# The opening of a two-layer hybrid trunk: first modulation on TensorE, norms applied tile by tile, convolution shifted later

## The chip, the core and the metric

The kernel runs on one core of one Trainium2 chip. The metric is device microseconds for one execution. Engines are called by their names in the profile: PE is TensorE (matmul), DVE is VectorE, ACT is ScalarE, POOL is GpSimd, SP is SyncE, which here only issues DMAs.

## The reference, cut to what matters

The trunk has two layers over 1024 latent tokens and 256 context tokens of 1024 channels. Layer 0 mixes tokens by a Conformer convolution module, layer 1 by attention; each is followed by a SwiGLU block. The change lies in layer 0, up to its second pointwise product.

```python
mod_x = (silu(c) @ w_mod[0] + b_mod[0]); mod_c = silu(c_ctx) @ w_mod[0] + b_mod[0]     # 6 x 1024 each
sh, sc, g, shf, scf, gf = split(mod, 6)                    # per stream
h  = rmsnorm(x, norm_g[0, 0]) * (1 + sc) + sh              # same for ctx with mod_c
u  = h @ w_pw1 + b_pw1                                     # 1024 -> 2048
a, gt = split(u, 2); u = a * sigmoid(gt)
u  = depthwise_conv(u, width 31) + b_dw                    # along the tokens of each stream
u  = silu(layernorm(u, ln_g, ln_b))
y  = u @ w_pw2 + b_pw2
x  = x + g * rmsnorm(y, norm_g[0, 1])
```

## The kernel before

**Tiling.** Channels lie on the 128 partitions, in KT = 8 tiles; tokens lie along the free axis in three pieces, C (256 context tokens), L and R (512 latent tokens each). Every large product runs in three matmuls on operands split in a high and a low part (wh·xh, wh·xl, wl·xh; L403 to L405 in `pw1`). A weight tile of 128x1024 is loaded by an SP DMA (L132), cast to its high part on ACT (L133), and the low part is a subtraction on DVE (L137) or POOL (L139). `split` does the same for activations: ACT L145, DVE L148.

**Opening.** Modulation chunk f is 128 of the 6144 outputs. On PE (`mod_pe`, L209 to L219) a chunk is eight K steps over a raw 512 KB weight tile, then a copy, a small transpose and a bias on ACT. On DVE (`mod_dve`, L226 to L243) a chunk is a multiply-and-reduce of the transposed raw tile (L241) for each of the two streams. Before the first product the kernel needs the chunks k (shift) and 8+k (scale), k = 0..7. It makes the eight shifts and the scale of k = 0 on PE, and the seven other scales on DVE. The raw tiles for PE lie in six slots of the buffers T4 and T5.

**Norms.** `norm_in` squares a piece (on ACT, L294), sums the squares over channels on PE (L297), takes an inverse root on DVE (L279 to L287, after L316), broadcasts it over the partitions by PE transposes (L323), and applies it: DVE L343 scales a tile, ACT L348 adds the shift and rounds to the high part, DVE L349 makes the low part. The three pieces are done one after the other, in program order.

**Blocks.** The loop over k = 0..7 runs `pw1(k)`: for each piece 48 matmuls, a sigmoid on ACT (L411) and a gate on DVE (L412) into `u`. `pw1` yields four times per piece, twelve times per k. After pieces C and R, eight DMAs on SP's queue (L421) regroup `u` into rows of 16 channels by 8 token phases (`U`, in buffer KB), and `split` makes `uh`, `ulo` (buffer HS) from it. The convolution is a generator, `conv`: group q = 8k+g is 15 matmuls of 162 columns (L464) against a weight map that DVE expands one group ahead (L444); three groups share a PSUM bank and are evicted by ACT (L469); after a block's last group two DMAs on ACT's queue store it to DRAM (L473) and DVE adds it into a running sum (L476, L478). Between the yields of `pw1` the loop calls `next(cg)`, from yield 18 on and at two yields of three. What is left of the 64 groups runs after the loop. Other yields step the second modulation (chunks 16 to 47), on DVE.

**Layer norm and pw2.** `ln` loads a piece of the stored convolution (SP, L499), subtracts the mean (PE L487, DVE L503), sums squares, scales (DVE L511), applies Silu (ACT L513). `pw2` (L517 to L529) is the second product; its matmuls stand at L156 to L158.

**What sets the order.** Each engine runs its own queue in order. A scheduler builds the queues from the program order and priorities; `later(n)` sinks PE instructions by n steps. `set_banks` names the PSUM banks of each kind. SP's queue is strictly in order, and a DMA there waits for its buffer ahead of everything behind it. Stores after the convolution, and nothing else in this part, go through ACT's queue.

Of the kernel before, what the change touches and what calls it, by code (L numbers as in the profile page):

```python
# [15 lines left out]
P = 128  # L16
# [17 lines left out]
PE_SCALE = (0,)  # L34
# [21 lines left out]
class Kern:  # L56
# [164 lines left out]

    def mod_dve(self, l, fs, cr, raws, junk):
# [3 lines left out]
        nc.sync.dma_start(cr.rearrange("p s d -> p (s d)"), self.a["crow"].to_broadcast([P, 2048]))  # L226
        nc.scalar.activation(cr, cr, AF.Silu)
# [62 lines left out]
    def sq_pe(self, ps, src, k, n):  # L290

        nc = self.nc
        sq = self.sb(n)
        nc.scalar.activation(sq, src, AF.Square)  # L294
        J = n // P
        for j in range(J):
            nc.tensor.matmul(ps[:, j:j + 1], lhsT=sq[:, j * P:(j + 1) * P], rhs=self.c["ones"],  # L297
                             start=k == 0 and j == 0, stop=k == KT - 1 and j == J - 1)

    def stat(self, acc, n, rs=True, kind="st", sums=None):  # L300
# [4 lines left out]
        ps = self.bank(kind) if sums is None else sums  # L305
        v = self.tiny([P, 16], "nv")
        parts = [(0, n // P, P)] + ([(n // P, J, rem)] if rem else [])
        for j in range(J if sums is None else 0):
# [50 lines left out]
    def norm_in(self, l, src_dram, tags, c0, c1, box, xt=None, kind="st", pe=False):  # L359
# [9 lines left out]
        if pe:  # L369
            ps = self.bank(kind)  # L370
            for k in range(KT):
                self.sq_pe(ps, xt[:, k, :], k, n)
                yield 0.1
            pb = self.stat(None, n, kind=kind, sums=ps)
        else:
            acc = self.acc(n)
            for k in range(KT):
                self.sq_acc(acc, xt[:, k, :], k)
                yield 0.1
            pb = self.stat(acc, n, kind=kind)  # L380
# [9 lines left out]
    def pw1(self, k, hs):  # L390
# [5 lines left out]
        for b, (c0, c1) in PIECES.items():  # L396
# [21 lines left out]
            if b != "L":  # L418
                u0, u1 = (0, CTX) if b == "C" else (CTX, TOK)
                for g in range(CG):  # L420
                    nc.sync.dma_start(self.U[:, g, o:o + nn], u[16 * g:16 * g + 16, u0:u1])  # L421
# [4 lines left out]
            yield  # L426

# [21 lines left out]
    def conv(self):  # L449

        nc, c = self.nc, self.c
        for q in range(KT * CG):
            k, g = divmod(q, CG)
            uh, ul, v = self.uh[k % 2], self.ulo[k % 2], self.v
            self.conv_maps(q + 1)
            h = g % 3
# [14 lines left out]
            if g == CG - 1:  # L471
                for d, o0, nn in ((self.vc[k], 0, NC_), (self.vl[k], 2 + NC_, NL)):
                    nc.scalar.dma_start(d.rearrange("g q n -> q g n"), v[:, :, o0:o0 + nn])  # L473
# [17 lines left out]
    def ln(self, b, ytag, stags, box):  # L491
# [4 lines left out]
        cv = self.T(ytag, [P, KT, n])  # L496
        for k in range(KT):
            d = (self.vc if b == "C" else self.vl)[k].rearrange("g (c s) n -> (g c) (s n)", s=PH)
            nc.sync.dma_start(cv[:, k, :], d[:, 512:] if b == "R" else d[:, :n])  # L499
# [356 lines left out]
    def build(self):  # L856
# [4 lines left out]

        mg = self.mod_dve(0, [8 + k for k in range(KT) if k not in PE_SCALE], *self.mod_room("HS", "KB"))
        gC = self.norm_in(0, a["xT"], ("HR", "T1", "T1"), *PIECES["C"], hs["C"], pe=True)
        self.set_banks(mm=[0, 1, 2], md=[3, 4, 7], st=[5, 6])
        b1 = self.cp.tile([P, KT], F32, tag="b1", name="b1")
        nc.vector.tensor_scalar(out=b1, in0=c["bmod"][:, 0, 8:16], scalar1=1.0, scalar2=None, op0=ALU.add)
# [5 lines left out]
        for k in range(KT):  # L872
# [9 lines left out]
            for s in range(2):  # L882
                if not onpe:
                    next(mg)
# [316 lines left out]
```

## Time and profile before

| | |
|---|---|
| median of 3 runs | 3191.86 us (3185.87 to 3194.25) |
| the profiled execution | 3192.76 us, span 3191.0 us |
| mean granted PE clock | 0.957 |
| busy: PE, DVE, ACT, POOL | 92%, 60%, 37%, 11% of the span |
| share of the chain that ended last | PE 35%, DVE 5%, DMA 2%, ACT 2% |

Times inside an execution are counted from the span's start, which is shorter than the execution's own time by 1.76 us. The layer's convolution module is over at about 600 us of the span; everything after (the rest of layer 0, and layer 1) is the same code in both kernels. A line of the trace's timeline gives the start, the busy time, the engine, the source line, the operation with its tiles, xN where N of them follow one another, and in brackets the idle time ahead of it with what ended it. "PEclk" is the granted clock as a share of full speed.

### The profile page before, as it was taken

The numbers are of one execution on the slowest core, as the hardware profiler recorded it, in microseconds if no ns is written. First come the engines' busy times: TensorE is split into PE (matmuls) and PEld (weight loads), VectorE is DVE, ScalarE is ACT, GpSimd is POOL, SyncE is SP. The second block draws the span as 40 slices with busy tenths as digits, with TensorE's granted clock in tenths as the row PEclk, the third lists the DMA queues.
The fourth block names the chain that finished last, engine by engine and source line by source line (L and its number), as shares of the span: only waits on it lengthen the run. The fifth ranks groups of instructions, "written<-read, shape, count | busy, mean of one in ns | idle before, by whom it ended". The sixth has DMA issues, their size and how long they took to land. (4 is left out here: it accounts for less than half of the span.)

```text
span 3191.0 us, 39121 instructions
## 1 busy us (share of the span) xinstructions
PE 2949.1 (92%) x15231; PEld 2467.8 (77%) x15231; DVE 1907.5 (60%) x3034; ACT 1193.0 (37%) x1859; POOL 354.1 (11%) x188
## 2 busy tenths in 40 slices
PE   7899978899999999999967799998999999899997
PEld 5789977788888887787856577776777778778886
DVE  5777667762333369855475689856656653663335
ACT  4211226432112232233332478754544543332222
POOL 0000000000000012222221100011111112222222
PEclk8899969999999999999988899998999999999998
DMA  6344333422122147623333411122122233343332
GB/s 231 109 130 117 77 103 113 158 86 66 61 66 66 60 154 242 254 94 107 119 111 127 148 53 60 52 90 88 62 80 78 63 103 108 126 145 99 93 99 73
DMA packets 170794, 340.68 MB, mean 107 GB/s; under 512 B 30448, under 2 KB 83824, under 8 KB 169328
## 3 DMA queue, kind: packets, MB, share of 16 engines
q1 hardware_dynamic: 153824, 332.72, 32.3%
q10 hardware_dynamic: 16784, 5.47, 0.7%
q8 instruction: 119, 1.95, 0.3%
q14 instruction: 67, 0.55, 0.1%
HBM read 290.94 MB, written 41.94 MB: 104 GB/s over the span
## 5 line engine op out<-in xcount | busy, mean ns | idle before, releaser
L158 PE MATMUL ps<-T,wl 128*128 128x512 f32 (+1 forms) x2256 | 847.2, 376 | 36.1 <-DVE wl L137 34.7
L156 PE MATMUL ps<-T,wh 128*128 128x512 f32 (+1 forms) x2256 | 847.7, 376 | 11.1 <-ACT wh L133 5.7
L157 PE MATMUL ps<-T,wh 128*128 128x512 f32 (+1 forms) x2192 | 818.9, 374 | 1.4 <-DVE T L148 1.3
L133 ACT CAST wh<-wr 128x1024 fp32r<-128x1024 f32 x348 | 365.4, 1050 | 1078.8 <-PE ps L157 833.5
L139 POOL TENSOR_TENSOR wl<-wr,wh 128x1024 fp32r<-128x1024 f32 x123 | 302.7, 2461 | 2441.6 <-ACT wh L133 2232.3
L137 DVE TENSOR_TENSOR wl<-wr,wh 128x1024 fp32r<-128x1024 f32 x225 | 282.1, 1254 | 403.2 <-ACT wh L133 396.3
L158 PEld LDWEIGHTS ps<-T,wl 128*128 128x128 f32 x2256 | 431.8, 192 | 111.6 <-DVE wl L137 38.2
L156 PEld LDWEIGHTS ps<-T,wh 128*128 128x128 f32 x2256 | 432.1, 192 | 84.3 <-ACT wh L133 5.9
L157 PEld LDWEIGHTS ps<-T,wh 128*128 128x128 f32 x2192 | 419.0, 191 | 71.1 <-DVE T L148 2.8
L157 PE MATMUL ps<-HS,wh 128*128 128x512 f32 (+1 forms) x784 | 308.2, 393 | 3.0 <-DVE HS L148 3.0
L803 DVE TENSOR_TENSOR T<-ps,T 128x512 fp32r<-128x512 f32 x320 | 216.9, 687 | 126.6 <-ACT T L802 125.9
L156 PE MATMUL ps<-HS,wh 128*128 128x512 f32 (+1 forms) x720 | 282.0, 393 | 3.6 <-DVE sm L612 3.6
L158 PE MATMUL ps<-HS,wl 128*128 128x512 f32 (+1 forms) x720 | 282.3, 393 | 3.0 <-DVE wl L137 3.0
L802 ACT CAST T<-ps 128x512 fp32r<-128x512 f32 x320 | 186.1, 586 | 194.2 <-PE ps L799 170.6
L799 PE MATMUL ps<-cst,T 128*128 128x128 f32 x1100 | 193.8, 277 | 30.1 <-DVE T L803 30.0
L636 DVE TENSOR_TENSOR T<-ps,T 128x512 f32<-128x512 f32 (+1 forms) x168 | 110.3, 663 | 159.7 <-PE ps L158 158.9
L799 PEld LDWEIGHTS ps<-cst,T 128*128 128x128 f32 x1100 | 132.7, 142 | 79.8 <-DVE T L803 61.0
L787 DVE TENSOR_SCALAR_CACHE_REDUCE T<-ps,rq 128x1280 f32<-128x1280 f32 x110 | 170.0, 1545 | 30.3 <-PE ps L781 25.4
L612 DVE TENSOR_TENSOR sm<-sm,ps 128x256 f32<-128x256 f32 (+1 forms) x88 | 54.6, 620 | 203.7 <-PE ps L158 203.7
L157 PEld LDWEIGHTS ps<-HS,wh 128*128 128x128 f32 x784 | 149.4, 191 | 34.2 <-DVE HS L148 4.0
L789 ACT ACTIVATE T<-T,mn 128x1280 f32<-128x1280 f32 x110 | 150.4, 1367 | 63.9 <-DVE T L787 63.6
L781 PE MATMUL ps<-KB,q 128*128 128x512 f32 (+1 forms) x576 | 144.0, 368 | 25.8 <-DMA KB<-ksd 16.5
(189 smaller groups left out, 4222.5 us busy)
## 6 DMA issues: line engine op xcount, KB each, us to landing
wr<-in_w SPq DMA_DIRECT2D x264, 512.0 KB
T<-in_wmodT SPq DMA_DIRECT2D x48, 512.0 KB
wr<-in_pw SPq DMA_DIRECT2D x40, 512.0 KB
KB<-in_wmodT SPq DMA_DIRECT2D x19, 512.0 KB
wr<-in_wmodT SPq DMA_DIRECT2D x16, 512.0 KB
wr<-in_wq SPq DMA_DIRECT2D x16, 512.0 KB
qsd<-sb SPq DMA_DIRECT2D x32, 256.0 KB
q<-qsd SPq DMA_DIRECT2D x32, 256.0 KB
```

The source lines that it names most:

```text
L133: nc.scalar.copy(hi, raw)
L137: nc.vector.tensor_tensor(lo, raw, hi.bitcast(F32), op=ALU.subtract)
L139: nc.gpsimd.tensor_tensor(lo, raw, hi.bitcast(F32), op=ALU.subtract)
L156: nc.tensor.matmul(out[:, :n], lhsT=wh, rhs=xh, start=k == 0, stop=False)
L157: nc.tensor.matmul(out[:, :n], lhsT=wh, rhs=xl, start=False, stop=False)
L158: nc.tensor.matmul(out[:, :n], lhsT=wl, rhs=xh, start=False, stop=k == nk - 1)
L781: nc.tensor.matmul(sc[:, k0:k0 + w], lhsT=q[:, h, :], rhs=kt[:, p * TOK + k0:p * TOK + k0 + w], start=p == 0, stop=p == 1)
L787: nc.vector.tensor_scalar(out=pt, in0=sc, scalar1=rq[:, h:h + 1], scalar2=None, op0=ALU.mult, op1=ALU.min, accum_out=mn)
L789: nc.scalar.activation(pt, pt, AF.Exp, bias=mn, scale=-1.0, accum_out=sums[:, 0, h:h + 1])
L799: nc.tensor.transpose(tp[:, h * P:(h + 1) * P], Ps[h][:, j * P:(j + 1) * P], c["ident"])
L802: nc.scalar.copy(ph, tp)
L803: nc.vector.tensor_tensor(pl, tp, ph.bitcast(F32), op=ALU.subtract)
```

## The change

- All sixteen chunks of shift and scale go to PE; their raw tiles lie in ten slots (T4, T5 and KB). No DVE chunk is left ahead of the first product.
- The pieces are loaded in four DMAs each. C's and L's squares and inverse roots are made first; C and L are applied tile by tile as each k's columns come. R's squares lie in between, from k = 4 on. All pieces now sum squares with `sq_acc` (ACT squares, DVE adds, PE sums at the end).
- Of the eight regrouping DMAs of a piece, the four with even g go through ACT's queue, the others through SP's.
- `split_u(k-1)` is called two yields into `pw1(k)`; the convolution starts at yield 22 instead of 18. After the loop three more groups run ahead of the last block's split.
- The convolved pieces are loaded back block by block from inside `conv` (`load_cv`), C's last block directly from SBUF.
- A Silu of one column on ACT stands after the loop. The PSUM banks of layer norm and `pw2` are four each.

```diff
 norm_in:
-        if pe:
-            ps = self.bank(kind)
-            for k in range(KT):
-                self.sq_pe(ps, xt[:, k, :], k, n)
...
+        acc = self.acc(n)
+        for k in range(KT):
+            self.sq_acc(acc, xt[:, k, :], k)
+            yield 0.1
+        pb = self.stat(acc, n, kind=kind)
 pw1:
-                    nc.sync.dma_start(self.U[:, g, o:o + nn], u[16 * g:16 * g + 16, u0:u1])
-            if b == "R":
-                if k + 1 < KT:
-                    self.pre.append(self.wload(a["pw1"][KT + k + 1]))
-                self.split(self.uh[k % 2], self.ulo[k % 2], self.U)
+                    (nc.sync if g % 2 else nc.scalar).dma_start(self.U[:, g, o:o + nn], u[16 * g:16 * g + 16, u0:u1])
+            if b == "R" and k + 1 < KT:
+                self.pre.append(self.wload(a["pw1"][KT + k + 1]))
 conv:
+            if q == CG * (KT - 1):
+                self.cvs = {}
+                for b, t in (("C", "KB"), ("L", "T4"), ("R", "T5")):
+                    self.cvs[b] = self.T(t, [P, KT, PIECES[b][1] - PIECES[b][0]])
+                    for j in range(KT - 1):
+                        self.load_cv(b, j)
 build:
-        mg = self.mod_dve(0, [8 + k for k in range(KT) if k not in PE_SCALE], *self.mod_room("HS", "KB"))
...
+        raws = [self.T(t, [P, 4, 1024]) for t in ("T4", "T5")] + [self.T("KB", [P, 2, 1024])]
+        raws = [raws[i][:, j] for j in range(4) for i in range(3) if j < raws[i].shape[1]]
         for k in range(KT):
             if k == 5:
                 self.pre += [self.wload(a["pw1"][0]), self.wload(a["pw1"][KT])]
+            self.mod_pe(k, raws[2 * k % len(raws)])
+            self.mod_pe(8 + k, raws[(2 * k + 1) % len(raws)])
...
+            if k == 1:
+                load_x("L")
+                self.cond_row(cr)
+                for _ in range(KT + 1):
+                    next(gL)
+                next(gC)
+            if k:
+                next(gC)
+                next(gL)
+            if k == 3:
+                xs["R"] = self.T("HS", [P, KT, 512])
+                load_x("R")
...
+            if k > 3:
+                for _ in range(2):
+                    next(gR)
...
         for k in range(KT):
             for i, _ in enumerate(self.pw1(k, hs)):
-                if 12 * k + i >= 18 and i % 3 != 1:
+                if k and i == 2:
+                    self.split_u(k - 1)
+                if 12 * k + i >= 22 and i % 3 != 1:
                     next(cg)
                 if i % 3 != 2:
                     next(modg, None)
+        self.set_banks(mm=[0, 1, 2, 3], cv=[4, 7], st=[5, 6])
+        nc.scalar.activation(self.tiny([P, 16], "nv")[:, :1], c["ones"], AF.Silu)
+        for _ in range(3):
+            next(cg)
+        self.split_u(KT - 1)
         for _ in cg:
             pass
```

**Where it moves instructions.** The first place is DVE's queue around piece R's inverse root, ahead of `pw1(1)`. Before, from R's sums to its first scaled tiles (nv, nq, nr, nh are the root's small tiles, HS holds R, sb is the scaled tile, HR the gate's result):

```order
L444 TENSOR_TENSOR T_610<-cwin,cst 128x640 x4
L316 TENSOR_SCALAR nv<-ps 128x4
L279 TENSOR_SCALAR nq<-nv 128x4
L283 TENSOR_SCALAR nh<-nv 128x4
L281 TENSOR_SCALAR nr<-nq 128x4
L412 SCALAR_TENSOR_TENSOR HR<-ps,cst,sm 128x512
L343 SCALAR_TENSOR_TENSOR sb<-HS,col_107,ps 128x512
```

The same place now (cwin is the convolution's window weights, T_622 a weight map, T_104 is piece L and T_282 its low part):

```order
L337 SCALAR_TENSOR_TENSOR sb<-T_104,col_109,ps 128x512
L310 TENSOR_SCALAR nv<-ps 128x4
L147 TENSOR_TENSOR cwin<-KB,cwin 128x320
L283 TENSOR_SCALAR nq<-nv 128x4
L287 TENSOR_SCALAR nh<-nv 128x4
L432 TENSOR_TENSOR T_622<-cwin,cst 128x640
L343 SCALAR_TENSOR_TENSOR T_282<-sb,mod_99,T_281 128x512
L285 TENSOR_SCALAR nr<-nq 128x4
L399 SCALAR_TENSOR_TENSOR HR<-ps,cst,sm 128x256
L337 SCALAR_TENSOR_TENSOR sb<-HS,col_109,ps 128x512
```

R's root now starts while piece L is still being scaled, with the window's split, L's last low part, C's gate and six weight maps (one is shown) among its steps; L's gate, which stood ahead of R's first tile, now stands behind R's last.

The second place is ACT's queue at the end of `pw1(0)`. Before, from the first 512-column sigmoid on (T_571 is R's high part, wh a weight's, HS the convolution's input):

```order
L411 ACT_TABLE_LOAD
L411 ACTIVATE sm<-ps,cst 128x512
L348 ACTIVATE T_571<-sb,mod_99 128x512 x8
L133 CAST wh<-wr 128x1024
L145 CAST HS<-KB 128x1328
```

The same place now, where T_584 is R's high part and KB<-HR the regrouping DMA of `u`:

```order
L398 ACTIVATE sm<-ps,cst 128x256
L342 ACTIVATE T_281<-sb,mod_99 128x512
L943 ACT_TABLE_LOAD
L943 ACTIVATE nv<-cst 128x1
L408 DMA KB<-HR 128x1x32 x4
L342 ACTIVATE T_584<-sb,mod_99 128x512 x2
L398 ACT_TABLE_LOAD
L398 ACTIVATE sm<-ps,cst 128x512
L342 ACTIVATE T_584<-sb,mod_99 128x512 x6
L408 DMA KB<-HR 128x1x128 x4
L132 CAST wh<-wr 128x1024
L144 CAST HS<-KB 128x1328
```

The one-column Silu, which the program has after the loop, stands here between C's and L's sigmoids with a table load of its own, and L's sigmoid has another behind it; four regrouping DMAs stand ahead of R's first tile and four ahead of the next weight's cast.

The third place is DVE's queue around the last block's split (HS<-KB), after the last `pw1` matmul. Before, from the last gate of `pw1(7)` on:

```order
L412 SCALAR_TENSOR_TENSOR HR<-ps,cst,sm 128x512
L444 TENSOR_TENSOR T_610<-cwin,cst 128x640 x4
L148 TENSOR_TENSOR HS<-KB,HS 128x1328
L148 TENSOR_TENSOR cwin<-KB,cwin 128x320
L444 TENSOR_TENSOR T_610<-cwin,cst 128x640 x6
L476 TENSOR_REDUCE sm<-HR 128x162
```

And now, from the same gate on:

```order
L399 SCALAR_TENSOR_TENSOR HR<-ps,cst,sm 128x512
L432 TENSOR_TENSOR T_622<-cwin,cst 128x640 x2
L147 TENSOR_TENSOR HS<-KB,HS 128x1328
L432 TENSOR_TENSOR T_622<-cwin,cst 128x640 x8
L147 TENSOR_TENSOR cwin<-KB,cwin 128x320
L432 TENSOR_TENSOR T_622<-cwin,cst 128x640 x6
L477 TENSOR_REDUCE sm<-HR 128x162
```

Two maps make one group. Behind the split stand now eight maps of groups that don't read it, and the window's split after them; on PE sixteen groups instead of thirteen follow the last `pw1` matmul.

More of the change, by code (lines that the diff above doesn't have):

```diff
@@ L495, in ln @@
         n = c1 - c0
[L496 to L499, printed above, removed]
+        cv = self.cvs[b]
         mean = self.mean(b)[:, :n]
@@ L944, in build @@
             pass
-        for _ in self.ln("R", tags["R"][0], tags["R"][1], sv["R"]):
+        for _ in self.ln("R", tags["R"][1], sv["R"]):
             pass
```

99 lines of the change are left out of this document (46 added, 53 removed).

## Prediction

> **What bounds the kernel now.** I read the page first, for what carries the whole.
>
> ```profile
> PE 2949.1 (92%) x15231; PEld 2467.8 (77%) x15231; DVE 1907.5 (60%) x3034; ACT 1193.0 (37%) x1859; POOL 354.1 (11%) x188
> ```
>
> PE is busy 92% of the span, so time can come only from stretches where PE waits or runs at a low clock. The change touches the first 600 us, so next I cut these with the windows view at the marks of the program: start of `pw1(0)`, start of `pw1(1)`, end of the last `pw1` matmul, end of the convolution, start of `pw2`. Columns: stretch, length, busy time of PE, PEld, DVE, ACT, POOL, granted PE clock, DMA share, GB/s.
>
> ```profile
> 0.00:36.29 36.29, 22.23 (x137) 16.36 (x137) 17.54 (x52) 13.95 (x36) 0.20 (x4) 1.00 0.76 282
> 36.29:123.89 87.60, 67.61 (x332) 56.02 (x332) 55.47 (x108) 33.40 (x55) 5.76 (x5) 0.72 0.37 120
> 123.89:409.66 285.77, 284.03 (x1775) 255.61 (x1776) 205.86 (x282) 54.84 (x100) 0.00 (x0) 0.98 0.43 115
> 409.66:449.80 40.14, 34.44 (x195) 33.93 (x194) 21.57 (x26) 6.48 (x15) 0.00 (x0) 0.63 0.55 158
> 449.80:469.90 20.10, 7.39 (x30) 6.48 (x30) 13.87 (x39) 6.90 (x16) 0.00 (x0) 0.50 0.23 66
> 469.90:600.00 130.10, 113.68 (x590) 96.70 (x591) 108.86 (x231) 83.25 (x144) 0.00 (x0) 0.95 0.38 126
> ```
>
> The third stretch, seven of the eight blocks, is full: PE 284.03 of 285.77 at clock 0.98. The second, one block, takes 87.60 at 0.72, and the fourth has PE at 0.63. The timeline says what PE waits for in the second.
>
> ```profile
> 70.65 1.22 PE L403 MATMUL ps<-T,wh 128*128 128x512 f32 x2 [1.59 <-ACT T L348]
> 96.61 0.16 DVE L316 TENSOR_SCALAR nv<-ps 128x4 f32<-128x4 f32 x1 [12.05 <-PE ps L297]
> 101.72 1.22 PE L403 MATMUL ps<-T,wh 128*128 128x512 f32 x2 [1.59 <-ACT T L348]
> 115.10 0.69 ACT L411 ACTIVATE sm<-ps,cst 128x512 f32<-128x512 f32 x1 [4.85 <-PE ps L405]
> 115.82 0.75 DVE L412 SCALAR_TENSOR_TENSOR HR<-ps,cst,sm 128x512 f32<-128x512 f32 x1 [1.10 <-ACT sm L411]
> 116.60 1.84 SPq L421 DMA_DIRECT2D KB<-HR  x3
> 118.55 0.52 SPq L132 DMA_DIRECT2D wr<-in_pw  x1
> 122.79 1.04 ACT L133 CAST wh<-wr 128x1024 fp32r<-128x1024 f32 x1 [7.00 <-DMA wr<-in_pw]
> 123.89 0.58 PE L403 MATMUL ps<-T,wh 128*128 128x256 f32 x1 [8.82 <-ACT wh L133]
> ```
>
> `pw1(0)` waits for each piece's norm in turn: L's product starts at 70.65, R's at 101.72, because R's sums end only at 96.61. Then comes a chain that is nobody's work: sigmoid, gate, three regrouping DMAs, the weight's DMA, its cast, and PE at 123.89 after 8.82 us idle.
>
> **The front.** The change orders the norms so that only the modulation is waited for. What it adds is traffic and PE work:
>
> ```profile
> 5.91 0.43 SPq L234 DMA_DIRECT2D HS<-in_wmodT  x1
> 18.81 0.33 SPq L209 DMA_DIRECT2D T<-in_wmod  x1
> 5.00:10.00 5.00, 4.17 (x21) 4.09 (x20) 0.00 (x0) 3.22 (x9) 0.00 (x0) 1.00 0.91 297
> 15.00:20.00 5.00, 4.15 (x26) 2.42 (x24) 0.31 (x2) 1.44 (x7) 0.00 (x0) 1.00 0.00 0
> 25.00:30.00 5.00, 3.80 (x32) 2.67 (x33) 4.96 (x12) 1.48 (x6) 0.00 (x0) 1.00 1.02 410
> L212 PE MATMUL ps<-T,cs 128*2 128x128 f32 x144 | 20.5, 302 | 4.5 <-DMA T<-in_wmod 4.5
> 77.20 0.39 PE L405 MATMUL ps<-T,wl 128*128 128x512 f32 x1
> 77.42 0.39 PE L403 MATMUL ps<-T,wh 128*128 128x512 f32 x1
> 100.16 2.06 DVE L343 SCALAR_TENSOR_TENSOR sb<-HS,col,ps 128x512 f32<-128x512 f32 x3 [0.55 <-PE ps L323]
> 102.14 2.07 DVE L349 SCALAR_TENSOR_TENSOR T<-sb,mod,T 128x512 fp32r<-128x512 f32 x3
> 113.43 1.23 DVE L241 CUSTOM_DVE_ANT_0 ps<-wr,HR 128x1024 f32<-128x1024 f32 x1
> ```
>
> Today SP's queue stands still from 6.3 to 18.8, while a raw slot is in use (0 GB/s in the window at 15 us), and moves 410 GB/s where it runs. With ten slots I see no such stop. Up to the last chunk the new queue carries sixteen raw tiles (8.4 MB by the code's shapes), the pieces (5.2), the condition rows (1.0) and the first two weights (1.0): 15.7 MB, at 410 GB/s 38 us. I add 5 for a slow start (the first rows are below 410), so the last chunk lands at 43 to 44. A chunk costs PE 20.5/9 = 2.3 us (144 matmuls were nine chunks), so two behind the last landing end at 48; columns and the last tiles of C and L (0.69 + 0.69 each on DVE, 2.06/3 and 2.07/3, and an ACT step) end near 54. L's 48 matmuls at the pitch 77.20 to 77.42, 0.22 us, then take 10.6: 65.
>
> R's root runs beside this, its steps between the window's split and six maps, and is ready at about 64. R's eight tiles cost DVE 8 x 1.38 = 11.0 us: 75, and `pw1(0)` ends at 76. Ahead of R's gate on DVE stand three chunks of the second modulation, 1.23 each and 0.1 for the small step behind it: 4.0, which puts the gate at 79 to 80. From the gate to PE took 123.89 - 115.82 = 8.1. On SP's queue three regrouping DMAs still stand ahead of the weight's, so I keep it: `pw1(1)` starts at 88 instead of 123.89, **-36**. Bounds: without the wait for the three chunks and with R's root done as L's product ends it is 80 (-44); if R's product meets the half clock (0.43 a matmul, 48 of them 20.5 instead of 10.6) it is 97 (-27).
>
> Two more table loads come into this stretch, since the scheduler takes the one-column Silu to the front.
>
> ```profile
> 58.75 1.28 ACT L411 ACT_TABLE_LOAD   x1
> 60.05 0.47 ACT L411 ACTIVATE sm<-ps,cst 128x256 f32<-128x256 f32 x1
> ```
>
> A load took 1.28 and the next instruction followed 0.02 later: 2.6 for both, of ACT time beside DVE's tiles, which pace here. I price it at nothing; uncovered it is 2.6. The Trainium skill ("ScalarE: Activation LUTs", What ACT_TABLE_LOAD costs) adds 1.38 us of drain to each switch, which would make it 5.3; the trace shows no such gap.
>
> **The full stretch.** Convolution from yield 22 on moves three of its 51 groups behind the loop.
>
> ```profile
> 179.59 1.75 PE L464 MATMUL ps<-HS,T 128*128 128x162 f32 x13 [1.74 <-DVE T L444]
> 182.08 0.63 PE L405 MATMUL ps<-T,wl 128*128 128x512 f32 x1
> 182.50 0.63 PE L403 MATMUL ps<-T,wh 128*128 128x512 f32 x1
> 185.48 1.80 PE L464 MATMUL ps<-HS,T 128*128 128x162 f32 x15
> 423.68 1.57 PE L464 MATMUL ps<-HS,T 128*128 128x162 f32 x5 [5.68 <-DVE T L444]
> ```
>
> Five groups ran from 409.66 to 423.68 - 5.68 = 418.00, so one is 1.67: -5.0. At 179.59 PE waited 1.74 us for the first split and then worked at half clock (pitch 0.42) until about 184.6; with the later start I take half of these 4 us back, -2. Together **-7** (-5 if the wait stays, -10 if it goes and another late eviction with it).
>
> The other new thing here is that half of the regrouping DMAs move to ACT's queue. There they wait for the gate on DVE, with evictions (L463), casts and sigmoids queued behind. The page of ACT in this stretch is 54.84 of 285.77 busy, so I cost it at nothing; what it costs without that cover is a rival.
>
> **The tail.** What follows the last `pw1` matmul, E = 409.66:
>
> ```profile
> 412.46 5.04 SPq L421 DMA_DIRECT2D KB<-HR  x8
> 419.52 1.30 ACT L145 CAST HS<-KB 128x1328 fp32r<-128x1328 f32 x1 [8.42 <-DMA KB<-HR]
> 420.85 1.54 DVE L148 TENSOR_TENSOR HS<-KB,HS 128x1328 fp32r<-128x1328 f32 x1 [5.48 <-DMA T<-vl]
> 435.00:440.00 5.00, 5.00 (x26) 5.00 (x25) 1.73 (x3) 0.59 (x3) 0.00 (x0) 0.50 0.34 112
> ```
>
> Eight DMAs take 5.04 to issue, then land; the split's two halves and a map follow; PE starts again at E + 14.0, and the eight groups left run to 449.80 at clock 0.50, 26.1/8 = 3.27 each. Now sixteen groups follow E. The issues are shared by two queues, so half of 5.04 goes and the split's first map comes at E + 11.5. The order has three more groups ahead of the split for cover, but their maps stand behind the split on DVE: only four groups have theirs ahead. PE runs 4 x 1.67 = 6.7, idles 4.8, and the other twelve run at half clock: 11.5 + 12 x 3.27 = E + 50.7 against E + 40.1, **+10.5**.
>
> The Trainium skill ("TensorE: Matmul & The Clock Gate", Part 1: The HAM clock gate) says that about 3.4 us of sustained work lift the gate. By it twelve groups would be cold for two of them only. The row at 435 disagrees: PE busy 5.00 of 5.00, eleven us after the wait, and the clock 0.50.
>
> **Layer norm and `pw2`.** The mean and L's subtractions move ahead of C's sums, with the pieces loaded earlier.
>
> ```profile
> 469.90 1.01 PE L156 MATMUL ps<-T,wh 128*128 128x256 f32 x3 [3.18 <-ACT T L145]
> 501.95 0.58 PE L158 MATMUL ps<-T,wl 128*128 128x256 f32 x1 [7.74 <-DVE wl L137]
> ```
>
> DVE gets L's tiles into C's chain, which makes `pw2`'s first matmul later by about 5, but PE then stands 7.74 us for a low weight part behind DVE's work in any case. I take **0**: -4 if L's early work shortens the wait, +8 if the second wait stays whole behind a later start. The changed banks and the early loads have their buffers free and cost nothing here; a load that waited for T4 or T5 on SP's queue would hold the `pw2` weights behind it, which is in the +8.
>
> **The sum**, against the profiled execution (3192.76 us; the median of the three runs, 3191.86, is 0.9 lower): -36 - 7 + 10.5 + 0 = -32.5, so 3160.
>
> **The rivals.**
>
> *The tail stays at full clock.* The conditions for the half clock are one wait in the trace; the 4.8 us idle is shorter than 5.68, and at 179.59 full clock was back within 5 us, among 512-column matmuls. All twelve groups warm: E + 11.5 + 20.0 = E + 31.5, -8.6 instead of +10.5, total 3141. By the skill's rule of 3.4 us it is about 2 more. Against: the 26 us at 0.50.
>
> *The front gains less.* R's product meets the half clock (the second stretch has 0.72 today, and PE waits for each of R's tiles again), -27, and `pw2` is late by 4: -27 - 7 + 10.5 + 4 = -19.5, 3173.
>
> *ACT's queue, slower than before.* Each block puts eight DMA issues on ACT, 0.63 each by the row at 412.46: 5.0 us, and each first one waits for a gate behind DVE's maps. With two convolution banks, an eviction held that long stops PE, which loses the wait and then some 4 us of half clock, as at 179.59. At 7 us a block, eight blocks make +56, 3192.76 - 32.5 + 56 = 3216. It decides from 32.5/8 = 4.1 us a block. Against: ACT has 80% of that stretch free.
>
> *It doesn't do what it says.* The loads stop for a raw slot as now (18.81 - 6.34 = 12.5 us), R meets the half clock (9), the tail costs 10.5, `pw2` 8, and the full stretch gives 7: -36 + 12.5 + 9 + 10.5 + 8 - 7 = -3, 3190, no difference.
>
> **How the numbers follow.** A measurement of this kernel can tell about 0.3%, 9.6 us, from no change. Forecast 0.50 (its own range 3150 to 3174), tail at full clock 0.19, the smaller front 0.14, ACT's queue 0.11, no difference 0.06. Faster: 0.83, same: 0.06, slower: 0.11. The range leaves out the last two, 0.17. Low end: 3141 with the front at -44 and the full stretch at -10, 3130. High end: 3173 with `pw2` at its full +8 (4 more), the full stretch at -5 (2) and the table loads uncovered (2.6), 3182.
>
> **What would show it.** In the changed trace: L's product near 54, R's gate near 80 behind three chunks, `pw1(1)` at 88; no stop of SP's loads before 43; PE full at clock 0.98 up to the last `pw1` matmul near 367; then four groups, an idle of about 4.8, twelve groups at 0.50, and the convolution's end near 417; `pw2` from about 440. It is wrong if `pw1(1)` starts after 100, if evictions wait for regrouping DMAs on ACT and PE for these, if the tail's clock is 1.00, or if `pw2`'s stretch is longer than 138.

## The result, and the profile after

Over 20 runs each the changed kernel takes 3186.03 us median (3180.15 to 3191.90), the kernel before 3193.05 (3185.87 to 3195.81): ratio 0.998, 95% interval 0.9973 to 0.9987. That is 7 us faster; the forecast was 3160 with a range of 3130 to 3182, and the 7 us lie within what the prediction called no change. The profiled execution of the changed kernel took 3188.66 us (span 3186.8, clock 0.956).

The windows view of the changed kernel, cut at the same marks as before (start of `pw1(0)`, of `pw1(1)`, end of the last `pw1` matmul, of the convolution, first matmul of `pw2`):

```profile
0.00:43.21 43.21, 28.10 (x187) 18.91 (x188) 19.91 (x62) 20.82 (x54) 0.48 (x5) 0.88 0.96 368
43.21:100.67 57.46, 45.03 (x260) 34.59 (x259) 44.70 (x89) 26.84 (x58) 4.60 (x5) 0.92 0.28 74
100.67:377.30 276.63, 276.63 (x1731) 248.78 (x1731) 202.94 (x276) 53.94 (x97) 0.00 (x0) 0.99 0.43 117
377.30:429.40 52.10, 46.85 (x240) 46.48 (x239) 26.53 (x32) 7.62 (x19) 0.00 (x0) 0.57 0.42 125
429.40:454.40 25.00, 8.96 (x38) 8.19 (x38) 19.86 (x50) 11.32 (x23) 0.00 (x0) 0.50 0.14 43
454.40:600.00 145.60, 125.28 (x624) 106.05 (x624) 118.01 (x254) 89.36 (x153) 0.00 (x0) 0.91 0.39 131
```

To see the rest of the program I take the 55th cast of a weight tile as a mark, which both kernels do in the same place of the same code. Its row in the timeline of the kernel before and of the changed one:

```profile
724.27 1.06 ACT L133 CAST wh<-wr 128x1024 fp32r<-128x1024 f32 x1 [1.97 <-PE ps L157]
```

```profile
707.73 1.05 ACT L132 CAST wh<-wr 128x1024 fp32r<-128x1024 f32 x1 [1.95 <-PE ps L156]
```

| stretch, us | before | changed | difference | forecast |
|---|---|---|---|---|
| start to `pw1(1)` | 123.89 | 100.67 | -23.2 | -36 |
| to the last `pw1` matmul | 285.77 | 276.63 | -9.1 | -7 |
| tail, to the convolution's end | 40.14 | 52.10 | +12.0 | +10.5 |
| to `pw2`'s first matmul | 20.10 | 25.00 | +4.9 | 0, with the next |
| to the 55th cast | 254.37 | 253.33 | -1.0 | |
| from there to the span's end | 2466.7 | 2479.1 | +12.3 | not in the sum |
| span | 3191.0 | 3186.8 | -4.2 | -32.5 |

So 32 us are won up to the last `pw1` matmul, 16 are given back by the 55th cast, and 12 more in code that the change doesn't touch. A stretch of that code in which PE is busy all the time, at clock 1.00 in both kernels, shows fewer matmuls in the same 100 us (second column, xN). Before, then changed:

```profile
2900.00:3000.00 100.00, 100.00 (x441) 82.58 (x440) 40.12 (x33) 26.27 (x32) 22.32 (x10) 1.00 0.31 95
```

```profile
2900.00:3000.00 100.00, 100.00 (x435) 81.47 (x435) 40.33 (x34) 25.80 (x31) 21.57 (x9) 1.00 0.31 96
```

"Pitch" below is the mean distance of the starts of neighbouring 512-column matmuls from 2800 us on, worked out from the trace's records: 227.7 ns before, 230.4 in the changed kernel. "Rest" is the stretch from the 55th cast to the end, E the end of the last `pw1` matmul, the tail the time from E to the convolution's end.

### The profile page after: what moved, and what is told of

Read it like the earlier page. It is cut to its first block, busy times and chain, and to the rows that moved or that the text cites. A ratio compares the mean times of both kernels' runs of the same rounds, so it can differ in the third digit from the quotient of the medians.

```text
span 3186.8 us, 39120 instructions
## 1 busy us (share of the span) xinstructions
PE 2954.3 (93%) x15210; PEld 2461.8 (77%) x15210; DVE 1899.3 (60%) x3026; ACT 1193.6 (37%) x1879; POOL 352.9 (11%) x188
## 3 DMA queue, kind: packets, MB, share of 16 engines
q8 instruction: 119, 1.95, 0.3%
## 5 line engine op out<-in xcount | busy, mean ns | idle before, releaser
L157 PEld LDWEIGHTS ps<-T,wl 128*128 128x128 f32 x2256 | 432.9, 192 | 113.5 <-DVE wl L136 35.4
```

The source lines that it names most:

```text
L157: nc.tensor.matmul(out[:, :n], lhsT=wl, rhs=xh, start=False, stop=k == nk - 1)
```

## The experiments

**Is the slower rest the run or the kernel?**

> The changed kernel once more, unchanged, for a second profile. In the first pair of profiles it is 32.5 us ahead at the last pw1 matmul, 16.5 ahead at 600 us and only 4.2 at the end, with a 512-column matmul every 230.3 ns after 2800 us where the kernel before had 227.8. Theory A, the pitch of the later matmuls differs from execution to execution: the front and the tail repeat within 2 us (pw1(1) at 100.7, convolution's end at 429), but the pitch after 2800 us comes out anywhere from 227.5 to 231, and the time follows it. Theory B, the shorter opening itself makes the later matmuls slower: the pitch is again above 229.5 and some 12 us are lost again after 600 us.

3184.99 us; `pw1(1)` at 100.2, tail 52.2, rest 2478.8, pitch 230.38. It repeats, so it belongs to the kernel. What the change alters for untouched code is the memory: it no longer allocates `b1` (32 bytes), and it names the large tiles in another order, so that HR lies at byte 20064 of a partition instead of 84800, HS at 149536 instead of 20096, T4 at 56928 instead of 52032, and so on.

```diff
+        nc.gpsimd.memset(self.cp.tile([P, KT], F32, tag="b1", name="b1"), 0.0)           # shift_back, old_places
+        for t in ("HS", "KB", "T4", "T5", "HR", "T1", "T6", "T2", "T3"):                 # old_places
+            nc.gpsimd.memset(self.T(t, [P, 1]), 0.0)
```

> The changed kernel dropped a constant tile of 32 bytes a partition (b1), which stood ahead of all large tiles, so that every buffer behind it (weights wr, wh, wl, the tiles T, HS, KB) lies 32 bytes lower: multiples of 64 before, 32 above one now. Here an unused tile of 32 bytes stands in its place and nothing else changes; the order of the large tiles in the memory stays the changed one. Theory A, the offset makes the 512-column matmuls of the unchanged later code slower: after 2800 us their pitch comes back from 230.4 ns to 228 or less, the rest of the program (from the 55th weight cast to the end) takes 2466 to 2470 us instead of 2475 to 2479, the time falls by 8 to 12. Theory B, it is the new places of the large tiles against each other: pitch and rest stay. Theory C, it is the chip's state or the earlier course: they stay as well.

> The changed kernel with the 32 bytes back and the large tiles (HS, KB, T4, T5, HR, T1, T6, T2, T3) at the addresses that they have in the kernel before; POOL writes one column of each at the start for that. Theory A (the offset alone): as with the 32 bytes alone, rest 2466 to 2470, pitch after 2800 us 228 or less. Theory B (the places of the large tiles): only here the rest comes back to about 2467 and the pitch to 227.7, time 10 to 12 less than the changed kernel's. Theory C (state or course): rest stays at 2475 to 2479, pitch at 230.4.

The 32 bytes alone: 3185.15 us, ratio to before 0.9982 (0.9972 to 0.9992), rest 2473.4, pitch 230.39. With the old places: 3181.66, ratio 0.9972 (0.996 to 0.9984), rest 2468.2, pitch 227.65. Theory B holds for the pitch, theory A is out. The first stage was 2 us later for the writes, which hid part of the gain. The reverse, on the kernel before, with 32 bytes more:

> The kernel before, with one unused tile of 32 bytes more, so that every large buffer lies 32 bytes off a multiple of 64. Theory A (the offset): its later matmuls slow down to a pitch near 230, the rest takes 2474 to 2480 us instead of 2466.7, the time rises by 8 to 12. Theory B (places of the large tiles against each other) and C: pitch 227.7, rest 2466 to 2468, time unchanged within 2.

3194.99, ratio 1.0008 (0.9999 to 1.0018), rest 2467.1, pitch 227.68: nothing. Then the names without the writes, in the changed kernel, and the changed kernel's order in the kernel before:

```diff
+        for t in ("HR", "T6", "T4", "T5", "KB", "T1", "T2", "T3", "HS"):                 # before_new_places
+            self.T(t, [P, 1])
```

> The changed kernel with the large tiles in the order that they have in the memory of the kernel before, without the 32 bytes and without the writes at the start (the tiles are only named early). If the places of the large tiles make the later matmuls slow, the rest takes 2467 to 2470 us and the pitch after 2800 us is 227.7; the front stays as in the changed kernel (pw1(1) at 100 to 101, where the writes had cost 2), and the time falls by 9 to 12, to about 3175. If the earlier kernel's gain came from the writes or the 32 bytes together, the pitch stays at 230.4 and the time at 3186.

> The kernel before with its large tiles named early in the order that they have in the memory of the changed kernel (HR first, HS last); all instructions stay. If the places alone make the later matmuls slower, the pitch after 2800 us is 230.4 ns instead of 227.7, the rest takes 2475 to 2480 us instead of 2467, and the time rises by 8 to 13, to about 3203. If the changed kernel's slower rest had another cause, nothing moves by more than 2.

With the old places the changed kernel takes 3178.74, ratio 0.9955 (0.994 to 0.997), rest 2470.0, pitch 227.63. The kernel before with the new places takes 3208.11 and is slower: ratio 1.004 (1.0025 to 1.0055), rest 2481.3, pitch 230.54. Its instructions are the same, only addresses differ. The windows of the two show it in the count of matmuls, `old_places_free` first, `before_new_places` behind it:

```profile
2900.00:3000.00 100.00, 100.00 (x441) 82.42 (x440) 39.81 (x36) 26.28 (x31) 21.59 (x9) 1.00 0.31 99
```

```profile
2900.00:3000.00 100.00, 100.00 (x434) 81.30 (x434) 35.16 (x29) 26.27 (x32) 21.56 (x9) 1.00 0.31 96
```

The rest scatters between profiles even at the same pitch (2473.4 to 2481.3 at 230.4 ns, 2466.7 to 2473.3 at 227.7); the pitch doesn't. With the old order the changed kernel's rest is 9.1 shorter and its median 7.3 less, so the places carry some 7 to 9 of the 12.3; the other 3 are within that scatter.

The pitch by what the matmuls read, worked out from the same records from 2800 us on, shows which products are hit: with the new places those that read one of the T tiles against a high weight (wh) go from 227.1 to 231.7 ns, against a low one (wl) from 226.8 to 232.5, while those that read HS get faster, from 228.9 and 229.4 to 227.4 and 226.5. These are the kernel before and the changed one; `old_places_free` and `before_new_places` give the same figures for their order of tiles within 0.3. Which other tile disturbs the T tiles, and how, was not tried.

**The tail.** In the changed kernel PE runs three groups behind E, not four, and waits for an eviction. The timelines of PE and of ACT:

```profile
377.11 5.15 PE L458 MATMUL ps<-HS,T 128*128 128x162 f32 x45
387.47 41.89 PE L458 MATMUL ps<-HS,T 128*128 128x162 f32 x195 [5.21 <-ACT HR L463]
```

```profile
380.08 2.83 ACTq L408 DMA_DIRECT2D KB<-HR  x4
385.25 1.30 ACT L144 CAST HS<-KB 128x1328 fp32r<-128x1328 f32 x1 [6.54 <-DMA KB<-HR]
386.45 0.96 ACT L463 ACTIVATE HR<-ps,cst 128x162 f32<-128x162 f32 x3
```

The eviction stands behind the split's cast, which waits for the regrouping DMAs. First I took the split off ACT and DVE:

```diff
-        self.split_u(KT - 1)
+        hi, lo = self.uh[1], self.ulo[1]
+        nc.gpsimd.tensor_copy(hi, self.U)
+        nc.gpsimd.tensor_tensor(lo, self.U, hi.bitcast(F32), op=ALU.subtract)
```

> The changed kernel with the last block's split (high part and low part) on POOL instead of ACT and DVE, so that nothing in ACT's or DVE's queue waits for the regrouping DMAs. Theory A, the evictions held behind the split's cast on ACT open a 5.2 us gap on PE, and the gap puts the convolution at half clock: the sixteen groups run with a gap under 2 us at full clock, the convolution ends 27 to 31 us after the last pw1 matmul instead of 52, and the time falls by about 20 us. Theory B, a stretch of convolution groups alone sinks to half clock whether or not there is a gap: the end comes at 45 to 52 us, the time falls by 0 to 6.

3181.89 us (3167.84 to 3189.39), ratio 0.9964 (0.9951 to 0.9977); tail 47.9. A gap is left, behind the four DMA issues on ACT, and behind it the half clock:

```profile
384.08 41.08 PE L458 MATMUL ps<-HS,T 128*128 128x162 f32 x195 [1.80 <-ACT HR L463]
386.00:425.00 39.00, 39.00 (x184) 38.94 (x183) 21.62 (x23) 4.05 (x12) 4.41 (x2) 0.50 0.38 117
```

This looks like theory B, but the gap isn't zero. (One of the ten runs took 3167.84 at a mean clock of 0.968, the others 0.957 to 0.960; it was not profiled.) So next with five PSUM banks for the convolution, `cv=[4, 7, 0, 1, 2]` instead of `[4, 7]` behind the loop:

> As with the split on POOL, where 1.8 us of gap were left (PE waited for a PSUM bank, whose eviction stood behind four regrouping DMAs on ACT) and the clock still fell right behind them; here the convolution also has five banks instead of two after the loop, so that PE waits for no eviction. Theory A, any gap of some 2 us tips the clock, and without one the convolution keeps it: idle under 0.5 us, clock 1.00, the tail takes 27 to 30 us instead of 52, time 20 to 25 less than the changed kernel's. Theory B, convolution groups alone sink to half clock by themselves some microseconds after the last pw1 matmul: no idle, but the tail is 42 to 48 and the time falls by 5 to 9.

3182.70, ratio 0.9967 (0.9954 to 0.998), tail 48.7, gap 1.9: my expectation that PE waits for no eviction was wrong, and the reason is in the code. `set_banks` sets the ring's counter to zero, the change calls it behind the loop, and so groups 48 to 50 and 51 to 53 both get bank 4. Naming the ring `[7, 0, 1, 2, 4]` heals it:

> The bank ring starts anew where the banks are named after the loop, so groups 48 to 50 and 51 to 53 both got bank 4 and PE waited for the eviction, with the split on POOL too (1.8 us). Here the changed kernel has the split on POOL and the ring named as 7, 0, 1, 2, 4: 51 to 53 go to bank 7. Theory A (a gap tips the clock): PE runs from the last pw1 matmul on with under 0.5 us idle, the clock stays 1.00, the tail takes 27 to 30 us and the time falls by 20 to 25. Theory B (convolution groups alone sink to half clock): no idle, but clock 0.50 from some point of the tail on, 40 to 48 us, time 5 to 10 less.

3174.80, ratio 0.9945 (0.9927 to 0.9962). PE's timeline, and two windows:

```profile
376.74 13.53 PE L458 MATMUL ps<-HS,T 128*128 128x162 f32 x120
392.22 0.43 PE L458 MATMUL ps<-HS,T 128*128 128x162 f32 x2 [1.95 <-DVE T L432]
392.86 24.04 PE L458 MATMUL ps<-HS,T 128*128 128x162 f32 x118 [0.22 <-DVE T L432]
```

```profile
385.00:389.00 4.00, 4.00 (x39) 4.00 (x37) 3.91 (x5) 1.43 (x4) 3.47 (x2) 1.00 0.87 263
397.00:401.00 4.00, 4.00 (x21) 4.00 (x21) 3.96 (x6) 0.06 (x1) 0.00 (x0) 0.50 0.54 156
```

Convolution alone holds full clock for eight groups (120 matmuls, 13.5 us); then PE waits 1.95 us for the next map, and the other eight groups take 24.7, at 0.50 in the second window. Tail 40.0, against 48.7 with the same five banks in the other order.

The wait comes from the split on POOL. Group 56 is the first that reads it, and the map that group needs stands beside POOL's subtraction:

```profile
388.26 3.13 POOL L948 TENSOR_TENSOR HS<-KB,HS 128x1328 fp32r<-128x1328 f32 x1
388.44 3.63 DVE L432 TENSOR_TENSOR T<-cwin,cst 128x640 fp32r<-128x640 f32 x1
```

The map took 3.63 us where its neighbours take 0.81, and ended 0.7 behind the subtraction. A map of 0.81 would have been there at 389.3, but PE, free at 390.27, would still have had to wait for the subtraction until 391.4 (estimates from these rows).

Either the gap or the time could have tipped the clock, so the last test, on the best kernel so far, fills the gaps with matmuls that nobody reads:

```diff
+            if q in (CG * (KT - 1), CG * (KT - 1) + 2):
+                for i in range(14 if q % CG else 12):
+                    nc.tensor.matmul(self.ps[:, 3, :], lhsT=self.cw[(q - 1) % 3][0][:, :P], rhs=self.xfill, start=True, stop=True)
...
```

The edit does one thing more, which these lines leave out: on DVE the running sum of block 6 stands behind group 57 instead of the block's last group. In the queue that puts it one map earlier (behind fifteen maps of the tail instead of sixteen).

> The kernel combined_2, with the two places of the tail where PE waits for maps or for the split (ahead of groups 56 and 58) filled with 12 and 14 matmuls of 512 columns, whose results nobody reads (into PSUM bank 3). In combined_2 eight groups ran at full clock, then a gap of 2.0 us at group 56 put the other eight at 0.50. Theory A, the gap tips the clock: with the fill it stays 1.00, the eight last groups take 13 to 15 us instead of 25.5 beside the 5.9 of the fill, the tail is 32 to 35 instead of 41.4, the time 6 to 9 less, 3146 to 3150. Theory B, the clock falls after some 15 us of convolution whatever comes between: the fill is paid in full, the tail is 44 to 48, the time 3158 to 3162.

```profile
374.80 13.53 PE L470 MATMUL ps<-HS,T 128*128 128x162 f32 x120
388.16 2.95 PE L465 MATMUL ps<-T,T 128*128 128x512 f32 x12
390.94 3.48 PE L470 MATMUL ps<-HS,T 128*128 128x162 f32 x30
394.26 3.42 PE L465 MATMUL ps<-T,T 128*128 128x512 f32 x14
397.51 10.17 PE L470 MATMUL ps<-HS,T 128*128 128x162 f32 x90
```

```profile
374.80:407.70 32.90, 32.88 (x267) 31.65 (x265) 28.15 (x31) 6.63 (x17) 5.95 (x2) 1.00 0.66 199
```

The clock stays 1.00 to the end, the tail is 32.7 with 6 us of filling in it, against 41.4 in `combined_2`. Theory A's forecast came true, and theory B's, that the clock falls after some 15 us whatever comes between, did not. (The filling isn't convolution, so it could keep the clock up by its own work as well as by closing the gap; convolution alone for longer than 13.5 us was not run.) In the profile the blocks took 284.0 us instead of 280.7, in a part that the edit leaves alone: PE waits for maps there eight times, 4.8 us in all, instead of five times and 3.0, and the clock is 0.50 once more, from 315 to 318. Why the maps are late there is open; the time fell by less than the tail.

**The convolution's place.** The start at yield 18, the split behind its DMAs, no groups ahead of the last split:

```diff
-                if k and i == 2:
-                    self.split_u(k - 1)
-                if 12 * k + i >= 22 and i % 3 != 1:
+                if i == 11:
+                    self.split_u(k)
+                if 12 * k + i >= 18 and i % 3 != 1:
...
-        for _ in range(3):
-            next(cg)
-        self.split_u(KT - 1)
```

> The changed kernel with the convolution put back: from yield 18 on, the split right behind the block's regrouping DMAs, no groups ahead of the last split. Theory A, the shift gains in the blocks what it loses in the tail: the tail from the last pw1 matmul to the convolution's end is about 40 us instead of 52, the seven full blocks take 283 to 286 instead of 276, and the time is within 5 us of the changed kernel's. Theory B, the shift is a net gain of its own: the blocks lose the 9 us and the tail gains nothing, the time is 9 us more. Theory C, it is a net loss: the blocks stay at 276 to 278 and the time falls by 10 or more.

3178.96, ratio 0.9958 (0.9943 to 0.9973); the blocks take 283.4, the tail 42.2. The shift wins 7 in the blocks and loses 10 in the tail: as written a loss of some 3 to 7 us, between theories A and C. With the split on POOL and the ring healed the shifted kernel has 276.3 + 40.0, 9 us less than 283.4 + 42.2. The ring alone is worth 8.7 of that tail (48.7 against 40.0, split on POOL in both), so with both mended the shift pays; what the ring costs with the split on ACT and DVE was not tried.

**The second modulation in block 0.**

```diff
-                if i % 3 != 2:
+                if k and i % 4 != 3:
                     next(modg, None)
```

> The changed kernel with the second modulation (on DVE) stepped from block 1 on only, at nine yields of a block instead of eight. Its raw tiles take every second turn of the two weight buffers, so theory A: in block 0 the weights of pw1(1) wait for a buffer that DVE reads from until 93.6, and R's gate stands behind three chunks. With the steps gone from block 0 the first weight is there when R's product ends, PE's 10.3 us of idle shrink to 0 to 6, pw1(1) starts at 90 to 96 instead of 100.5, and the time falls by 4 to 10. Theory B, the regrouping DMAs ahead of the second weight on SP's queue hold the block as well: pw1(1) starts early, but PE waits as long for the second weight, and the last pw1 matmul stays within 2 us of 377.

What it is about, in the queues of DVE and SP of the changed kernel: DVE reads a raw tile in a weight buffer (wr) until 93.6, and the weight's DMA is issued at 94.41, behind three regrouping DMAs that hold SP's queue until 94.3.

```profile
92.37 1.22 DVE L245 CUSTOM_DVE_ANT_0 ps<-wr,HR 128x1024 f32<-128x1024 f32 x1
```

```profile
94.41 0.53 SPq L131 DMA_DIRECT2D wr<-in_pw  x1
```

3178.96, ratio 0.996 (0.9945 to 0.9975). The first weight is loaded long before R's product ends, `pw1(1)` starts at 91.0 without a wait, E is 370.4 instead of 377.3: theory A.

**Layer norm's banks.** `set_banks(mm=[0, 1, 2, 3, 4, 7], st=[5, 6])` as before:

> The changed kernel with the PSUM banks of layer norm and pw2 as in the kernel before (six and two instead of four and four). Theory A, with four banks for sums DVE weaves piece L's subtractions and sums into C's inverse root, which makes pw2 late: from the convolution's end to pw2's first matmul 20 us instead of 25, of which the 55th weight cast, at 704 to 708, keeps 0 to 4. Theory B, the early work on L is paid back in pw2: pw2's first matmul comes 5 earlier, but the 55th weight cast is as late or later, and the time rises by 0 to 4.

C's inverse root in the changed kernel, and `pw2`'s first matmul in this one:

```profile
442.99 1.01 PE L305 MATMUL ps<-cst,acc 128*128 128x1 f32 x4 [4.51 <-DVE acc L329]
451.94 0.66 PE L317 MATMUL ps<-cst,nr 128*128 128x128 f32 x2 [7.94 <-DVE nr L291]
```

```profile
449.56 1.01 PE L155 MATMUL ps<-T,wh 128*128 128x256 f32 x3 [3.17 <-ACT T L144]
```

The stretch is 20.1 again: the banks made `pw2` 5 us late. The 55th cast comes at 702.6 (704.4 and 707.7 in the changed kernel's two profiles), so 2 to 5 of that are kept. Time 3183.88, ratio 0.9966 (0.9953 to 0.9979), not told apart from the changed kernel's.

**The front.** Three tries at why the modulation ends at 62 instead of 48. Half of the K steps (their sums are left out):

> The changed kernel with every second K step of the sixteen modulation chunks on PE left out (half of their matmuls; the modulation values are therefore not the full sums); loads and everything else stay. Theory A, PE's own queue (16 chunks, C's product and the waits between them) sets the end of the modulation at 62 us: it comes 12 to 20 us earlier, and pw1(1) starts at 82 to 90. Theory B, the landing of the raw tiles sets it: the end stays within 4 us of 62 and pw1(1) at 97 to 101.

The end came at 62.4, `pw1(1)` at 104.6, the time was 3191.34. More of C's product now stands ahead of the last chunks (the scheduler seems to count a chunk as cheaper), and PE, less busy, is at half clock longer: a mean clock of 0.74 from the first chunk to the last, against 0.87. Theory A fails in this form. R's load later (at k = 6, its squares with it):

> The changed kernel with piece R's load (2.1 MB, 5 us of DMA) moved behind 13 of the 16 raw modulation tiles instead of 8, and its squares with it. Theory A, the landing of the raw tiles paces the modulation: its end comes 3 to 5 us earlier than 61.5 to 62, at 57 to 59. Theory B, PE's queue (chunks, C's product, sums and transposes in one order, partly at half clock) paces it: the end stays at 60 to 63.

62.8, `pw1(1)` 103.9, 3193.37: theory B. Fourteen of the sixteen raw tiles were issued by 26.7 here, the last two no earlier than before (35.5), and PE still had six chunks to do at 45.4. C's product later (weights loaded at k = 7):

> The changed kernel with the first two weights of pw1 loaded two modulation steps later (at k = 7), so that the scheduler puts three of the last six modulation chunks ahead of C's first product on PE instead of behind it. Theory A, C's product (and the wait for its weights) in PE's in-order queue makes the modulation end late: its end comes 3 to 8 us earlier than 62, at 54 to 59; what that gives pw1(1) is 0 to 5 us, since C's product has then to be done behind it. Theory B, something else paces the last chunks: their end stays at 60 to 63.

59.7, `pw1(1)` 98.3, 3180.57: 2 us, less than expected; the scheduler still wove most of C's product in. What paces the chunks is settled this far: not the loads, and no single one of the pieces taken away. Each of the three is one execution.

**Together.** Old places, second modulation from block 1, split on POOL, five banks; then also the ring and the old layer norm banks:

> The changed kernel with three edits together: the large tiles at their old order, the second modulation from block 1 on, the last split on POOL with five convolution banks. If they add up: rest 2467 to 2470 (-10), last pw1 matmul at 370 (-7), tail 27 to 30 (-22) if the clock holds or 42 to 48 (-4 to -9) if not: 3147 to 3150, or 3160 to 3165. If the second modulation's steps, which now also fall into the last block, hold DVE's maps, the tail's share is lost: about 3170.

> The combined kernel (old places of the large tiles, second modulation from block 1 on, split on POOL, five convolution banks) with the ring named as 7, 0, 1, 2, 4 and with the old banks of layer norm and pw2. If the clock holds in the tail: 20 to 25 less than the combined kernel's 3167.6 plus 2 to 4 for layer norm, 3140 to 3146. If it falls anyway: 3160 to 3165.

`combined` takes 3167.55, ratio 0.9915 (0.9898 to 0.9931), with the tail at 48.2, as its ring still gives bank 4 twice. `combined_2` takes 3155.44, ratio 0.9883 (0.9867 to 0.9898), 39.7 us less than the kernel before beside it (3195.16). `tail_filled` takes 3151.30 (before: 3190.31), ratio 0.9869 (0.9848 to 0.989). Both beat the kernel before and the changed one; between the two the intervals overlap.

## Why the prediction was wrong, step by step

**The front, -36, measured -23.2.** The step "the last chunk lands at 43 to 44 ... so two behind the last landing end at 48" failed in its second half. The loads did run without a stop; the last raw tile was issued at 35.42. But PE still had six chunks to do at 46.7, not two. SP's and PE's timelines and three windows of the changed kernel:

```profile
35.42 0.33 SPq L208 DMA_DIRECT2D KB<-in_wmod  x1
```

```profile
9.71 5.21 PE L211 MATMUL ps<-T,cs 128*2 128x128 f32 x32 [9.71 <-DMA T<-in_wmod]
46.70 5.32 PE L211 MATMUL ps<-T,cs 128*2 128x128 f32 x32
60.10 1.91 PE L211 MATMUL ps<-KB,cs 128*2 128x128 f32 x16
100.67 0.58 PE L390 MATMUL ps<-T,wh 128*128 128x256 f32 x1 [10.32 <-ACT wh L132]
```

```profile
20.00:30.00 10.00, 5.83 (x30) 4.03 (x27) 6.78 (x24) 4.97 (x11) 0.00 (x0) 0.66 1.03 394
50.00:62.00 12.00, 12.00 (x97) 8.82 (x95) 7.95 (x17) 7.03 (x21) 0.00 (x0) 0.98 0.06 24
9.71:62.01 52.30, 45.28 (x310) 31.14 (x310) 28.14 (x79) 26.92 (x73) 4.68 (x2) 0.87 0.72 277
```

The same window for the chunks alone (L211; here the columns are PE and PEld):

```profile
9.71:62.01 52.30, 35.40 (x256) 23.08 (x256) 0.87 0.72 277
```

PE started at 9.7, stood 4 us between 20 and 30 at a mean clock of 0.66, and C's product lies between the chunks. I had costed the chunks behind the last landing and not PE's queue as a whole; sixteen chunks of 2.3 us from 9.7 on are 46.5 without anything else in the queue. The windows say what else there was: from the first chunk to the last PE was busy 45.3 of 52.3 us, the chunks are 35.4 of these, 2.2 each, so their price was right. The other 9.9 us of work (the sums and roots of the pieces, small transposes, part of C's product) and 7.0 us of idle are what the forecast left out. The loads moved only 24 GB/s from 50 on. From the modulation's end on the steps held: 28 us to the end of R's product in the forecast (48 to 76), 28 in the trace (62 to 100.67 - 10.32 = 90), and 10.3 of idle up to `pw1(1)`. That idle I took as SP's order; `second_mod_later` shows that the weight comes early when its buffer is free, and the idle goes with the chunks that held it.

**The full stretch, -7, measured -9.1.** Right. PE is busy 276.63 of 276.63, so the whole wait for the first split is gone, of which the forecast took half. The rival of ACT's queue did not come about there: no eviction held PE in the blocks.

**The tail, +10.5, measured +12.0.** The size was right, the mechanism partly: twelve groups at half clock behind a wait were forecast, thirteen came. I named DVE's maps; PE waited earlier, for an eviction, since the bank ring starts anew and gives bank 4 twice. That is in the diff, and I took the line for a repetition. The eviction stood behind the split's cast, which waits for the regrouping DMAs: the chain that the rival of ACT's queue names, in the tail instead of the blocks. So the size is right partly by luck: PE restarts at E + 10.2 instead of E + 11.5, with one group more to run cold. The rival of a tail at full clock was wrong for this kernel; in `tail_filled`, with the gaps filled, the clock did stay 1.00.

The Trainium skill ("TensorE: Matmul & The Clock Gate", Part 1: The HAM clock gate) has the clock back after some 3.4 us of sustained work; here PE worked 41.89 us without a pause behind the wait, at half clock. Nor is the Trainium skill's idle window of the same length before a fall (the same section) what the runs show: the clock fell behind gaps of 1.80 and 1.95 us.

**Layer norm and `pw2`, 0, measured +3.9.** Inside the range given (-4 to +8). The later start of 5 was named; it was not paid back by a shorter wait. The forecast put the changed banks at nothing, and `old_ln_banks` shows that they bring the 5: with the old ones the stretch is 20.1 again.

**The rest, not in the sum, +12.3.** The prediction said that code after about 600 us is unchanged, and took its time as unchanged. That step failed: the order in which the tiles are first named sets their addresses, and with them the pitch of the matmuls that read the T tiles. That is 7 to 9 of the 12.3; for the others no cause is shown.

Of the 28 us between forecast and the pair of profiles the front is 13, the rest 12, layer norm 4; the blocks (2 better) and the tail (1.5 worse) nearly cancel.

## What to carry to other kernels

A change that renames or reorders buffers moves addresses, and can slow code that it doesn't touch: compare the pitch of a stretch that should be equal before looking for a cause in the changed part. A line that sets up a ring again also sets its counter back; look at which slot the next user gets. When loads are no longer the bound, count everything that stands in PE's queue up to the mark, not only what is behind the last landing. Work moved to an idle engine can still hold up a busy one: look at the single instructions beside it, not at the mean.

## What the runs showed of the hardware that I had not expected

The place of the large tiles in the memory changes the pitch of 512-column matmuls by 1.2% (227.7 to 230.4 ns) at the same granted clock, with the same instructions, up for those that read a T tile and slightly down for those that read HS; 32 bytes of offset don't. The Trainium skill ("SBUF — State Buffer", SBUF: two separate sides) says that PE waits for no one there; the paired runs don't fit that, or the cause lies elsewhere than in a port.

Convolution groups of 162 columns hold full clock for at least 13.5 us when they come at it warm, and don't regain it in 41 to 42 us when they come at it behind a gap of 1.80, 1.87 or 5.21 us (`tail_on_pool`, `tail_no_gap`, the changed kernel). In the kernel before, 512-column matmuls regained it within 5 us of the wait at 179.59.

DVE waited for POOL in the last split. In all six profiles with the split on POOL one map took 3.36 to 3.67 us and ended 0.7 us behind POOL's subtraction; the maps after it took 0.81 again. In the changed kernel, with nothing on POOL, six maps in a row took 4.50:

```profile
388.04 4.50 DVE L432 TENSOR_TENSOR T<-cwin,cst 128x640 fp32r<-128x640 f32 x6
```
